# A two-layer hybrid backbone on one core: the places of layer 1's experts, its output rows, and the making of the first mixer's input

## The chip, the core and the metric

The kernel runs on one core of one Trainium2 chip, in one launch. The metric is the device time of that core in microseconds (us), the median of three runs. The engines are named as the profile names them: PE (TensorE, matrix products and transposes), DVE (VectorE), ACT (ScalarE), POOL (GpSimd) and SP (SyncE, which here issues the loads of the weights). PEld is the loading of a stationary operand into PE.

## The reference, cut to what matters

Two layers; layer 0 mixes with a gated recurrence, layer 1 with attention, and each is followed by a mixture of 16 experts of which every token takes two. Layer 0 works on 512 tokens (256 of the context and 256 of the image), layer 1 on the 256 of the image.

```python
def modulate(x, g, shift, scale):
    return rms_norm(x, g) * (1 + scale) + shift

def rglru_mixer(hx, hc, in_w, ...):            # layer 0; hx, hc are outputs of modulate
    gx_, ux = jnp.split(hx @ in_w, 2, axis=-1)
    ...
    log_a = -LRU_C * r * jax.nn.softplus(-lam) # lam: a learned vector, the same for all tokens
    ...

def grouped_moe(h, router_w, router_b, w1, w3, w2):
    probs = jax.nn.softmax(h @ router_w + router_b, axis=-1)
    ...                                        # the best of 4 groups, its best two experts
    y = jnp.zeros_like(h)
    for e in range(N_EXPERTS):
        y = y + gates[..., e:e + 1] * ((jax.nn.silu(h @ w1[e]) * (h @ w3[e])) @ w2[e])
    return y

# layer 1, last line
x = x + g_f * grouped_moe(hx, router_w, router_b, moe_w1[i], moe_w3[i], moe_w2[i])
```

D_MODEL is 1024, the experts' inner width 512. One weight matrix of one expert is 2 MB, so an expert is 6 MB in three tiles (w1, w3, w2).

## The kernel before, in words

**Weights.** SP issues all weight loads in a fixed list, each tile in two halves of 1 MB, with at most four halves in flight (`AHEAD`). A tile of weights goes into one of ten buffers in layer 1; `done(key)` gives a tile's buffer up and sends the next load of the list.

**Layer 1's experts** (`moe_`, `run`). The experts are worked one after the other at places 0 to 15, called `e` in the code. Places 0 to 3 hold experts 0 to 3, whose weights can be loaded before the router is done. The other twelve are ranked by how many tokens they got, and `ORDERS[1]` says which rank stands at which place from 4 on. `ROOM[1]` gives each rank its room: 160 rows for ranks 0 and 1, 32 for the rest, and `AGAIN` marks ranks 2 and 3, which get a further block of 128 rows under an `If` when they have over 32 tokens. Room of 160 is two blocks, one of 128 tokens and one of 32. From the reference, with these inputs, the router gives the places from 4 on 32, 29, 147, 19, 147, 16, 7 and 1 tokens; from place 12 on there are none, and their loads and work are skipped. No `If` finds over 32 tokens.

At each place PE does, in this order: `ups(e)` (w1 and w3, then the turning of the next expert's tokens), `downs(e-1)` (w2 of the place before), `flips(e)` (the transposes ahead of its own `downs`), and, if the next place has two blocks, the turning of its second block (`xh`). At place 11 `downs(10)` comes ahead of `ups(11)`. After `ups(e)` the buffers of w1 and w3 are given up, after `downs(e-1)` that of w2.

**Output rows.** `down` scales the product out of PSUM by gate and gain with DVE (L989) into a piece of `ys`, two tiles of 1024 columns (they are rows of the buffer `xr`), and POOL adds the piece to the output in DRAM by an indirect DMA (L995), a scatter. `row` picks the piece: a block of 128 rows takes the whole of `ys[(e + b) % 2]`, a block of 32 rows takes 256 columns of `ys[e % 2]`. A write into a piece waits until the scatter that reads the same bytes has landed. Each scatter waits until the one before it has landed, and holds POOL's queue meanwhile.

**The first mixer's input** (`modulate`). For each of 8 groups of 128 channels `k`, `m` is scale times value plus shift for 512 tokens, `hi` is `m` rounded to the narrower type `fp32r` and `lo` is what is left over, also in that type; PE then makes three products for each `k` (`mm3`: L182 with both high parts, L183 with `lo`, L184 with the low part of the weights). `m` is made by ACT, or by DVE where k is 1, 4 or 7; `hi` by DVE; `lo` by DVE or, for odd k, by POOL. `split` parts the weights in the same way: high part by DVE (L584), low part by POOL (L585). `lambda_terms` makes three small vectors out of `lam` with some thirty DVE instructions on 128x16 numbers and one `Exp` of ACT; the recurrence uses them for the first time in `back(0)`. In this stretch the order of PE, ACT and DVE is the order in which the code is written.

Of the kernel before, what the change touches and what calls it, by code (L numbers as in the profile page):

```python
# [12 lines left out]
AF = mybir.ActivationFunctionType  # L13
ALU = mybir.AluOpType
# [20 lines left out]
ADA_AT = [32, 34]  # L35


ORDERS = [[11, 0, 10, 1, 9, 2, 8, 3, 7, 4, 6, 5, 12], [2, 3, 0, 4, 1, 5, 6, 7, 8, 9, 10, 11]]
ROOM = [[192, 128, 96, 96, 96, 96, 64, 64, 64, 64, 64, 64, 32], [160, 160, 32] + 9 * [32]]

AGAIN = [[1, 2, 3, 4, 6], [2, 3]]
# [25 lines left out]
def base(i, k):  # L67

    return BASE if k < FIRST[i] else ROOM[i][ORDERS[i][k - FIRST[i]]]


def again(i, k):

    return k < FIRST[i] or ORDERS[i][k - FIRST[i]] in AGAIN[i]

# [12 lines left out]
def hybrid_kernel(ctx: ExitStack, tc: tile.TileContext, x, c, ctxt, c_ctx, ada_w, ada_b, norm_mix_w, norm_ffn_w,  # L88
# [3 lines left out]
    nc = tc.nc  # L92
# [77 lines left out]
    def take(key):  # L170
        return live[key][0]
# [106 lines left out]
    def vectors():  # L278
        pt = bank()
        nc.tensor.transpose(pt[:, 0:128], v1, ident)  # L280
        nc.tensor.transpose(pt[:, 128:256], v2, ident)
        nc.vector.tensor_copy(vt, pt[:, 0:256])
        init.close()
# [10 lines left out]
    def tables(pool):  # L294
        stage = pool.tile([128, C_COS - C_N], F32, name="stage", bufs=1)
        nc.gpsimd.dma_start(cst[:, 128:C_N], cf[:, 128:C_N])
        nc.gpsimd.dma_start(stage, cf[:, C_N:C_COS])
        nc.gpsimd.dma_start(rot, cf[:, C_COS:C_ALL])
        nc.gpsimd.dma_start(rw, router_w.rearrange("(k p) e -> p k e", p=128))
        nc.gpsimd.dma_start(rb, router_b.unsqueeze(0).to_broadcast([128, E]))  # L300
        nc.gpsimd.dma_start(qkw[:, 0, :], attn_q_norm_w.to_broadcast([128, 64]))
        nc.gpsimd.dma_start(qkw[:, 1, :], attn_k_norm_w.to_broadcast([128, 64]))
        for dst, at in ((lt_b, C_LT), (io_b, C_IO), (dup_b, C_DUP)):
            nc.vector.tensor_copy(dst, stage[:, at - C_N:at - C_N + dst.shape[1]])
        nc.vector.memset(ones_b, 1.0)
# [34 lines left out]
    def vec(i, m):  # L340
        return adT[i][:, m * 8:m * 8 + 8, :]

    def scale_vec(i, m, gain0, name):
        t = cp.tile([128, NK, 2], F32, name=name)
        g = vt[:, gain0 + i * 8:gain0 + i * 8 + 8].unsqueeze(2).to_broadcast([128, NK, 2])
        nc.vector.scalar_tensor_tensor(t, vec(i, m), 1.0, g, ALU.add, ALU.mult)
        return t
# [37 lines left out]
    def modulate(pool, xT, hi, lo, between):  # L385

        A = scale_vec(0, SC_M, 96, "am0")
        B = vec(0, SH_M)
        for k in range(NK):
            m = pool.tile([128, 512], F32, tag="m", name="m", bufs=3)  # L390
            for j in range(2):
                sl = slice(j * 256, j * 256 + 256)
                if k % 3 == 1:
                    nc.vector.tensor_scalar(m[:, sl], xT[:, k, sl], A[:, k, j:j + 1], B[:, k, j:j + 1], ALU.mult, ALU.add)
                else:
                    nc.scalar.activation(m[:, sl], xT[:, k, sl], AF.Identity, bias=B[:, k, j:j + 1], scale=A[:, k, j:j + 1])
            if k == 0:
                between()
            nc.vector.tensor_copy(hi[:, k, :], m)  # L399
            (nc.gpsimd if k % 2 else nc.vector).tensor_sub(lo[:, k, :], m, hi[:, k, :])  # L400

    yr0 = dp.tile([512, D], F32, name="yr0")

# [145 lines left out]
    def lambda_terms():  # L549
        nl, w, s, s2 = (sw[:, a, :] for a in range(4))  # L550
        nc.vector.tensor_scalar(nl, lam, -1.0, None, ALU.mult)
        nc.vector.tensor_tensor(w, nl, lam, ALU.min)
        nc.scalar.activation(w, w, AF.Exp)
        nc.vector.tensor_scalar(s, w, 2.0, None, ALU.add)
        nc.vector.reciprocal(s, s)
        nc.vector.tensor_mul(s, s, w)
        nc.vector.tensor_mul(s2, s, s)
        nc.vector.memset(k8, 1.0 / 17)
        for q in range(15, 0, -2):
            nc.vector.tensor_mul(k8, k8, s2)  # L560
            nc.vector.tensor_scalar(k8, k8, 1.0 / q, None, ALU.add)
        nc.vector.tensor_mul(k8, k8, s)
        nc.vector.tensor_scalar(k8, k8, 2.0, None, ALU.mult)
        nc.vector.tensor_scalar(nl, nl, 0.0, None, ALU.max)
        nc.vector.tensor_add(k8, k8, nl)
        nc.vector.tensor_scalar(k4, k8, 4.0, None, ALU.mult)
        nc.vector.tensor_scalar(k8n, k8, -8.0, None, ALU.mult)

    with tc.tile_pool(reuse_waits="tile", name="big0", bufs=1) as bp:
# [9 lines left out]
        def split(name, b):  # L579

            w = take((name, b // 4)).rearrange("p (k f) -> p k f", k=NK)[:, :, (b % 4) * 128:(b % 4) * 128 + 128]
            at = 2048 * (name == "ing")
            h, lo = (parts[:, at + z * 1024:at + (z + 1) * 1024].rearrange("p (k f) -> p k f", k=NK) for z in range(2))
            nc.vector.tensor_copy(h, w)  # L584
            nc.gpsimd.tensor_sub(lo, w, h)  # L585
            whi[name, b] = h, lo
            if b % 4 == 3:
                done((name, b // 4))
# [10 lines left out]
        with tc.tile_pool(reuse_waits="tile", name="n0", bufs=2) as n0, \  # L599
                tc.manual_schedule(engines={ET.PE, ET.Activation, ET.DVE}):  # L600
            ras = []
            normed(n0, yT, lambda: ras.append(ada_mm(0, 0, False)), lambda: None)
            ras.append(ada_mm(0, 1, False))
            vectors()
            for n in range(2):
                ada_sum(0, n, ras[n])

            hhi = wp.tile([128, 4096], F32R, tag="w", name="hhi").rearrange("p (k t) -> p k t", k=NK)
            parts = wp.tile([128, 4096], F32R, tag="w", name="parts")
            lambda_terms()  # L610
            ras = [ada_mm(0, n) for n in (2, 3)]
            for n in range(2):
                ada_sum(0, 2 + n, ras[n])
            modulate(n0, yT, hhi, hlo, lambda: split("in", 0))
            split("ing", 0)
            split_gates(0)
        with tc.tile_pool(reuse_waits="tile", name="m0", bufs=1) as mp:
# [64 lines left out]
            u = front(0)  # L682
            pg = product("ing", 0)
            split("in", 1)
            tables(mp)
            for b in range(8):
                r = gate_mm(b, *u[1:])
# [48 lines left out]
    def moe_(R, rp, early):  # L736
# [15 lines left out]
        if i == 0:  # L752
            xg, xh, sx, ys = places()
        with tc.tile_pool(reuse_waits="tile", name=f"r{i}", bufs=1) as q:
# [37 lines left out]
            m = small([128, C * E], "m")  # L792
# [47 lines left out]
        if i == 1:  # L840
            R.gf = rp.tile([128, D], F32, name="gf")
            xg, xh, sx, ys = places()
# [119 lines left out]
        def row(e, b, bk):  # L962

            if i == 1 and BLOCKS[bk] == BLOCKS[2]:

                return ys[e % 2][:, e // 2 % 4 * 256:]
            return ys[(e + b) % 2] if i or b == 0 else ys[2]

        def down(bk, aT, W2, ls, b, e):
# [699 lines left out]
def _constants():  # L1669
# [30 lines left out]
    for i in range(2):  # L1700
        k = FIRST[i]
        a[:, C_KEY + 16 * i:C_KEY + 16 * i + 16] = np.where(x < k, 65536 + 16384 * (k - 1 - x), E - 1 - x)
        a[:, C_RANK + 16 * i:C_RANK + 16 * i + 16] = list(range(k)) + [k + r for r in ORDERS[i]]
        a[:, C_ROOM + 16 * i:C_ROOM + 16 * i + 16] = [room(i, k) for k in range(E)]
# [32 lines left out]
```

## Time and profile before

| | us |
|---|---|
| median of three runs | 1001.43 |
| lowest and highest | 999.87, 1001.97 |
| the profiled execution, its own time | 1000.39 |
| its span, first to last instruction | 998.7 |
| PE busy | 854.6 (86%) |
| DVE, ACT, POOL busy | 488.5, 300.3, 253.8 |

The mean granted clock of PE is 0.933 of full speed. How to read the rows below: a row of the timeline has the start in us from the span's start, the time in us (of all its instructions together, pauses under 0.15 us included), engine, line, operation, out<-in, shape, count, and in brackets the idle time of the engine ahead of it and what ended it. Shapes tell the blocks of layer 1 apart: `128*128` is a block of 128 tokens, `128*64` one of 64, `128*32` one of 32. PE's lines in layer 1 are L946 (`ups`), L981 (`downs`), L928 (turning tokens), L958 (`flips`).

### The profile page before, as it was taken

Reading aid. Unit: us, or ns where it says so; the run is one execution under the profiler, and the core shown is the slowest. Engines: PE = TensorE matmul, PEld = TensorE weight load, DVE = VectorE, ACT = ScalarE, POOL = GpSimd, SP = SyncE. Lnnn points to the kernel's source line nnn. Section 1 sums busy time; section 2 is a strip of 40 time slices with the busy share of each in tenths; the row PEclk is TensorE's granted clock in tenths of the full one; section 3 lists DMA queues with packets and bytes.
Section 4 is the critical chain, followed back from the end, with each engine's and each line's share of the span. In section 5 each row is a group of like instructions: output and inputs, shape, how many; then the busy total and the mean of one; then the engine's idle time right before and its main releaser. Section 6 shows DMA issues by size and latency. Waiting matters only on the chain. (4 is left out here: it accounts for less than half of the span.)

```text
span 998.7 us, 17124 instructions
## 1 busy us (share of the span) xinstructions
PE 854.6 (86%) x6495; PEld 541.9 (54%) x6495; DVE 488.5 (49%) x1366; ACT 300.3 (30%) x549; POOL 253.8 (25%) x193
## 2 busy tenths in 40 slices
PE   3789899889996999999998953899999689799963
PEld 2356676575454555555654523688654556555632
DVE  1878797643147731222131106687842674334542
ACT  3346555674021211010011012557851311111100
POOL 2263233400002321111121106652430122313222
PEclk9799999998997999999999976799999799999987
DMA  9955974799515699999999985222949579999950
GB/s 346 357 175 191 389 264 169 261 386 380 211 67 213 239 361 385 363 363 359 351 337 372 374 288 175 84 73 80 354 162 399 204 290 370 378 386 367 382 184 9
DMA packets 126926, 277.11 MB, mean 277 GB/s; under 512 B 7673, under 2 KB 12889, under 8 KB 126816
## 3 DMA queue, kind: packets, MB, share of 16 engines
q1 hardware_dynamic: 116064, 253.77, 69.3%
q0 software_dynamic: 8880, 15.54, 6.7%
q10 hardware_dynamic: 1872, 6.37, 1.6%
q8 instruction: 64, 1.05, 0.4%
q14 instruction: 46, 0.38, 0.1%
HBM read 290.85 MB, written 14.81 MB: 306 GB/s over the span
## 5 line engine op out<-in xcount | busy, mean ns | idle before, releaser
L946 PE MATMUL up<-w,xg 128*64 128x256 f32 (+2 forms) x1888 | 171.7, 345 | 9.9 <-DMA w<-in_moe_w_dram 8.9
L946 PEld LDWEIGHTS up<-w,xg 128*64 128x64 f32 (+2 forms) x1888 | 107.2, 128 | 67.3 <-issue 31.8
L981 PE MATMUL py<-w,sx 128*32 128x256 f32 (+2 forms) x768 | 129.9, 528 | 6.0 <-DVE sx L960 3.4
L951 DVE TENSOR_TENSOR sx<-sx,up 128x256 f32<-128x256 f32 (+3 forms) x31 | 15.3, 494 | 174.3 <-PE up L946 97.5
L981 PEld LDWEIGHTS py<-w,sx 128*32 128x32 f32 (+2 forms) x768 | 45.7, 137 | 71.3 <-issue 55.8
L950 ACT ACTIVATE sx<-up 128x256 f32<-128x256 f32 (+3 forms) x31 | 12.2, 394 | 232.5 <-PE up L946 232.5
L585 POOL TENSOR_TENSOR parts<-w,parts 128x1024 fp32r<-128x1024 f32 x16 | 40.4, 2525 | 113.2 <-DVE parts L584 105.2
L995 POOL DMA_INDIRECT yr<-y,yi x21 | 33.4, 1591 | 121.4 <-DVE y L992 54.3
L531 PE MATMUL bank<-w,yT 128*128 128x512 f32 x128 | 57.3, 595 | 0.0
L182 PE MATMUL bank<-hhi,parts 128*128 128x512 f32 x128 | 52.9, 413 | 3.9 <-DVE hhi L399 3.8
L183 PE MATMUL bank<-hlo,parts 128*128 128x512 f32 x128 | 52.5, 410 | 4.2 <-DVE hlo L400 2.2
L184 PE MATMUL bank<-hhi,parts 128*128 128x512 f32 x128 | 51.9, 406 | 1.3 <-POOL parts L585 1.3
L918 POOL DMA_INDIRECT xg<-hr,gi x21 | 20.8, 991 | 125.9 <-DVE f L909 74.9
L946 PE MATMUL up<-w,xr 128*32 128x128 f32 (+2 forms) x736 | 51.2, 315 | 1.4 <-issue 0.9
L316 PE MATMUL bank<-w,st 128*32 128x512 f32 x384 | 46.5, 615 | 3.8 <-DMA w<-in_ada_w_dram 3.5
L946 PEld LDWEIGHTS up<-w,xr 128*32 128x32 f32 (+2 forms) x736 | 35.5, 120 | 14.5 <-issue 9.5
L933 ACT ACTIVATE xg<-tp 128x512 f32<-128x512 f32 x32 | 17.4, 594 | 84.7 <-PE tp L928 72.2
L992 DVE TENSOR_SCALAR y<-py,gt 128x512 f32<-128x512 f32 (+1 forms) x21 | 14.4, 687 | 56.7 <-PE py L981 55.1
L989 DVE SCALAR_TENSOR_TENSOR xr<-py,gt,gf 32x256 f32<-32x256 f32 (+2 forms) x44 | 24.4, 554 | 35.0 <-DMA out_dram<-xr,yi 19.6
L465 DVE TENSOR_TENSOR rt<-bank,gm 128x512 f32<-128x512 f32 x12 | 8.3, 692 | 66.9 <-PE bank L531 66.9
L531 PEld LDWEIGHTS bank<-w,yT 128*128 128x128 f32 x128 | 23.4, 190 | 25.7 <-issue 25.5
L1610 POOL TENSOR_SCALAR pe<-pe,mx 128x512 f32<-128x512 f32 x16 | 25.0, 1566 | 45.0 <-DVE mx L1605 29.7
(360 smaller groups left out, 1635.9 us busy)
## 6 DMA issues: line engine op xcount, KB each, us to landing
w<-in_moe_w_dram SPq DMA_DIRECT2D x192, 1024.0 KB
w<-in_ada_w_dram SPq DMA_DIRECT2D x48, 1024.0 KB
w<-in_lru_in_w_dram SPq DMA_DIRECT2D x8, 1024.0 KB
w<-in_attn_qkv_w_dram SPq DMA_DIRECT2D x6, 1024.0 KB
w<-in_lru_out_w_dram SPq DMA_DIRECT2D x4, 1024.0 KB
w<-in_attn_o_w_dram SPq DMA_DIRECT2D x4, 1024.0 KB
hr<-h ACTq DMA_DIRECT2D x6, 512.0 KB
yr<-zero POOLq DMA_DIRECT2D x4, 512.0 KB, 12.4
```

The source lines that it names most:

```text
L182: nc.tensor.matmul(pb, wh, xh, start=start, stop=False, skip_group_check=True)
L183: nc.tensor.matmul(pb, wh, xl, start=False, stop=False, skip_group_check=True)
L184: nc.tensor.matmul(pb, wl, xh, start=False, stop=stop, skip_group_check=True)
L316: nc.tensor.matmul(pa[32 * g:32 * g + 32, :], st[:, 4 * r + g, :], w[:, 4 * r + g, :], start=r == 0, stop=r == 1, skip_group_check=True, t ...
L531: nc.tensor.matmul(pb, src[:, k, n * 128:(n + 1) * 128], w[:, k, :], start=k == 0, stop=k == NK - 1)
L585: nc.gpsimd.tensor_sub(lo, w, h)
L918: nc.gpsimd.indirect_dma_start(out=dst[0:rows, :], out_offset=None, in_=hr[:, :], in_offset=bass.IndirectOffsetOnAxis(ap=idx[0:rows, :], a ...
L946: nc.tensor.matmul(pw[g * Tn:(g + 1) * Tn, at:at + fg], hT[:, k, t0:t0 + Tn], W[:, k, g * fg:(g + 1) * fg], start=k == 0, stop=k == NK - 1 ...
L981: nc.tensor.matmul(py[j * Tn:(j + 1) * Tn, 0:wd], aT[:, ao + q * 128 + g * Tn:ao + q * 128 + (g + 1) * Tn], W2[:, f, j * dg + h * 512:j * ...
L989: nc.vector.scalar_tensor_tensor(dst[ps, :], py[ps, 0:wd], gate[ps, :], R.gf[ps, at:at + wd], ALU.mult, ALU.mult)
L995: nc.gpsimd.indirect_dma_start(out=yr[:, :].rearrange("r (g f) -> (r g) f", g=G), out_offset=bass.IndirectOffsetOnAxis(ap=ls.yi[:, z, b:b ...
L1610: (nc.gpsimd if u else nc.vector).tensor_scalar(pe, pe, mx[:, 1:2], None, ALU.mult)
```

## The change

Four edits. `ORDERS[1]` begins with 2, 0, 3, 1, 4 instead of 2, 3, 0, 4, 1: places 4 to 8 now hold 32, 147, 29, 147 and 19 tokens. A block of 32 rows takes `ys[(e + b) % 2]`, so that the second block of an expert goes into the other tile than its first. In `modulate` ACT writes `hi` directly, DVE makes `m` for every k and all of `lo`; POOL makes none of it. `lambda_terms()` is called later in the code, behind the second `split("in", ...)`.

```diff
-ORDERS = [[11, 0, 10, 1, 9, 2, 8, 3, 7, 4, 6, 5, 12], [2, 3, 0, 4, 1, 5, 6, 7, 8, 9, 10, 11]]
+ORDERS = [[11, 0, 10, 1, 9, 2, 8, 3, 7, 4, 6, 5, 12], [2, 0, 3, 1, 4, 5, 6, 7, 8, 9, 10, 11]]
...
             for j in range(2):
                 sl = slice(j * 256, j * 256 + 256)
-                if k % 3 == 1:
-                    nc.vector.tensor_scalar(m[:, sl], xT[:, k, sl], A[:, k, j:j + 1], B[:, k, j:j + 1], ALU.mult, ALU.add)
-                else:
-                    nc.scalar.activation(m[:, sl], xT[:, k, sl], AF.Identity, bias=B[:, k, j:j + 1], scale=A[:, k, j:j + 1])
+                nc.scalar.activation(hi[:, k, sl], xT[:, k, sl], AF.Identity, bias=B[:, k, j:j + 1], scale=A[:, k, j:j + 1])
+                nc.vector.tensor_scalar(m[:, sl], xT[:, k, sl], A[:, k, j:j + 1], B[:, k, j:j + 1], ALU.mult, ALU.add)
             if k == 0:
                 between()
-            nc.vector.tensor_copy(hi[:, k, :], m)
-            (nc.gpsimd if k % 2 else nc.vector).tensor_sub(lo[:, k, :], m, hi[:, k, :])
+            nc.vector.tensor_sub(lo[:, k, :], m, hi[:, k, :])
...
-            lambda_terms()
             ras = [ada_mm(0, n) for n in (2, 3)]
...
             split("in", 1)
+            lambda_terms()
             tables(mp)
...
-                return ys[e % 2][:, e // 2 % 4 * 256:]
+                return ys[(e + b) % 2][:, e // 2 % 4 * 256:]
```

DVE at the start of the first mixer, before: the last of `lambda_terms` (L566, L567) is behind it; the last two `ada_sum` (L329, L330) and the scale vector `am` (L346) come first, then the first `split` and `modulate`.

```order
44 L329 TENSOR_REDUCE rs<-bank 128x8
45 L330 TENSOR_TENSOR adT_133<-rs,vt 128x8
46 L329 TENSOR_REDUCE rs<-bank 128x8
47 L330 TENSOR_TENSOR adT_133<-rs,vt 128x8
48 L346 SCALAR_TENSOR_TENSOR am_344<-adT_133,vt 128x16
49 L584 CAST parts<-w 128x1024
50 L399 CAST hhi<-m 128x512
51 L400 TENSOR_TENSOR hlo<-m,hhi 128x512
52 L394 TENSOR_SCALAR m<-yT,am_344,adT_133 128x256 x2
```

The same place after the change, with the lines three lower (L557 to L564 are now the end of `lambda_terms`, L581 the `split`, L397 `lo`).

```order
39 L329 TENSOR_REDUCE rs<-bank 128x8
40 L557 TENSOR_TENSOR k_140<-k_140,sw 128x16
41 L330 TENSOR_TENSOR adT_133<-rs,vt 128x8
42 L558 TENSOR_SCALAR k_140<-k_140 128x16
43 L346 SCALAR_TENSOR_TENSOR am_314<-adT_133,vt 128x16
44 L559 TENSOR_TENSOR k_140<-k_140,sw 128x16
45 L394 TENSOR_SCALAR m<-yT,am_314,adT_133 128x256 x2
46 L560 TENSOR_SCALAR k_140<-k_140 128x16
47 L562 TENSOR_TENSOR k_140<-k_140,sw 128x16
48 L563 TENSOR_SCALAR k_142<-k_140 128x16
49 L564 TENSOR_SCALAR k8n<-k_140 128x16
50 L581 CAST parts<-w 128x1024
```

The scheduler has not moved `lambda_terms` behind the products, as the code reads, but spread it between the `ada_sum` instructions, and `am` no longer stands behind all of it; the rounding of `hi` (L399) is gone from DVE.

PE at place 5 of layer 1, before: one block of 32 rows, then the `If` for more (L1150) and the turning of place 6.

```order
2723 L946 MATMUL up<-w,xg_13405 32x128 x64
2724 L1150 COMPARE_AND_BRANCH
2725 L928 MATMUL tp<-cst,xh 128x128 x8
2726 L946 MATMUL up<-w,xh 128x512 x16
2727 L958 MATMUL py<-cst,sx_13408 128x128 x4
2728 L1150 UNCONDITIONAL_BRANCH x2
2729 L928 MATMUL tp<-cst,xr 128x128 x8
```

The same place after the change.

```order
2719 L925 MATMUL tp<-cst,xh 128x128 x8
2720 L1089 TENSOR_LOAD cnk
2721 L1089 ISA x2
2722 L943 MATMUL up<-w,xg_13413 128x512 x16
2723 L943 MATMUL up<-w,xh 32x128 x64
2724 L925 MATMUL tp<-cst,xr 128x128
2725 L1020 UNCONDITIONAL_BRANCH
2726 L925 MATMUL tp<-cst,xr 128x128 x7
```

The expert with two blocks now stands here, and the `If` has gone to place 6.

POOL at the end of layer 1, before: the two scatters of place 8 (a row of 1024 columns, then pieces of 256), with gathers of later places between, then those of places 9, 10 and 11.

```order
2561 L995 DMA out_dram<-xr,yi 256x1024
2562 L995 DMA out_dram<-xr,yi 1024x256
2563 L1011 MEMSET xr 128x1024
2564 L918 DMA xr<-hr_13190,gi 32x1024
2565 L995 DMA out_dram<-xr,yi 1024x256 x2
2566 L1011 MEMSET xg_13405 128x1024
2567 L918 DMA xg_13405<-hr_13190,gi 32x1024
2568 L995 DMA out_dram<-xr,yi 1024x256
```

The same place after the change: the two scatters are now those of place 7.

```order
2555 L992 DMA out_dram<-xr,yi 256x1024
2556 L992 DMA out_dram<-xr,yi 1024x256
2557 L1008 MEMSET xr 128x1024
2558 L915 DMA xr<-hr_13198,gi 32x1024
2559 L992 DMA out_dram<-xr,yi 1024x256
2560 L1008 MEMSET xr 128x1024
2561 L915 DMA xr<-hr_13198,gi 32x1024
2562 L992 DMA out_dram<-xr,yi 1024x256 x2
2563 L1008 MEMSET xg_13413 128x1024
2564 L915 DMA xg_13413<-hr_13198,gi 32x1024
2565 L992 DMA out_dram<-xr,yi 1024x256
```

One more scatter and one more gather stand behind the last expert with two blocks.

## Rows read from the trace of the kernel before

**Rows 1.** Stretches of layer 1: start:end, length, busy by engine, PEclk, DMA, GB/s.

```profile
860.00:960.00 100.00, 92.60 (x1152) 56.18 (x1151) 39.54 (x151) 15.68 (x44) 25.40 (x22) 0.97 1.04 377
960.00:965.00 5.00, 0.03 (x2) 0.03 (x2) 2.34 (x7) 0.30 (x1) 0.20 (x1) 0.64 0.29 80
965.00:985.00 20.00, 15.37 (x239) 9.24 (x238) 11.92 (x55) 0.28 (x1) 8.34 (x7) 0.76 0.10 12
```

**Rows 2.** Timeline of PE, places 5 to 8 of layer 1.

```profile
865.49 4.18 PE L946 MATMUL up<-w,xg 128*32 128x128 f32 x128
...
872.60 1.30 PE L928 MATMUL tp<-cst,xr 128*128 128x128 f32 x5 [1.87 <-issue]
...
879.68 13.90 PE L946 MATMUL up<-w,xr 128*128 128x512 f32 x32
...
908.65 8.98 PE L981 MATMUL py<-w,sx 128*128 128x512 f32 x48
...
937.23 1.93 PE L981 MATMUL py<-w,sx 128*32 128x256 f32 x32
```

**Rows 3.** Timeline of PE, places 10 and 11 and the end.

```profile
954.30 3.82 PE L946 MATMUL up<-w,xr 128*32 128x128 f32 x128
...
964.97 0.22 PE L898 MATMUL pa<-r,dup_b 128*128 128x5 bf16 x3 [5.82 <-DVE r L883]
965.12 3.45 PE L981 MATMUL py<-w,sx 128*32 128x256 f32 x32
...
971.19 3.24 PE L981 MATMUL py<-w,sx 128*32 128x256 f32 x32 [2.33 <-DVE sx L960]
...
978.03 0.91 PE L946 MATMUL up<-w,xg 128*32 128x128 f32 x23 [0.30 <-issue]
...
981.61 3.41 PE L981 MATMUL py<-w,sx 128*32 128x256 f32 x32
```

**Rows 4.** Timeline of DVE: the second block of place 8.

```profile
962.56 1.96 DVE L989 SCALAR_TENSOR_TENSOR xr<-py,gt,gf 32x256 f32<-32x256 f32 x4 [9.55 <-DMA out_dram<-xr,yi]
```

**Rows 5.** Scatters: one link of the chain, then landings within 860:960 and from 960.

```profile
953.28 9.15 DMA out_dram<-xr,yi
...
DMA to landing us min/median/max: 7.4/7.4/7.5
...
DMA to landing us min/median/max: 3.8/3.8/3.9
```

**Rows 6.** Timeline of POOL: the last scatter.

```profile
987.50 1.59 POOL L995 DMA_INDIRECT out_dram<-xr,yi  x1 [6.07 <-DVEq L1233]
```

**Rows 7.** Timeline of all engines at the start of the first mixer.

```profile
34.49 0.66 PE L327 MATMUL bank<-cst,ra 128*128 128x128 f32 x4 [0.19 <-ACT ra L321]
...
37.04 0.18 DVE L346 SCALAR_TENSOR_TENSOR am<-adT,vt 128x16 f32<-128x16 f32 x1
...
37.68 0.69 DVE L584 CAST parts<-w 128x1024 fp32r<-128x1024 f32 x1 [0.47 <-DMA w<-in_lru_in_w_dram]
...
38.52 2.49 POOL L585 TENSOR_TENSOR parts<-w,parts 128x1024 fp32r<-128x1024 f32 x1 [32.28 <-DVE parts L584]
...
38.84 2.72 DVE L400 TENSOR_TENSOR hlo<-m,hhi 128x512 fp32r<-128x512 f32 x1
...
41.48 0.72 DVE L394 TENSOR_SCALAR m<-yT,am,adT 128x256 f32<-128x256 f32 x2
...
41.65 1.09 ACT L396 ACTIVATE m<-yT,adT,am 128x256 f32<-128x256 f32 x2 [2.32 <-DVE hlo L400]
...
47.15 0.69 DVE L400 TENSOR_TENSOR hlo<-m,hhi 128x512 fp32r<-128x512 f32 x1
...
51.41 1.67 POOL L400 TENSOR_TENSOR hlo<-m,hhi 128x512 fp32r<-128x512 f32 x1 [1.74 <-DVE hhi L399]
...
51.84 1.51 DVE L593 CAST g<-w 128x512 fp32r<-128x512 f32 x1
...
53.88 0.60 ACT L628 ACTIVATE upad<-bank 128x512 f32<-128x512 f32 x1 [6.25 <-PE bank L184]
```

## The prediction

> **What bounds the kernel now.** I read the share of the engines first, then the stretches of layer 1, then PE's timeline there, and last the start of the first mixer. PE is busy for 86% of the span, so an edit counts only where PE, or what follows its last product, waits. In layer 1 the stretches say which resource ends last [rows 1]: from 860 to 960 us the transfers run at 377 GB/s with a DMA share of 1.04 while PE is busy for 92.6 of 100 us; at 960 the weights are in (80 GB/s, then 12). Yet PE goes on until 985. So after 960 neither the weights nor PE's rate is the limit: between 960 and 965 PE is busy for 0.03 us, and between 965 and 985 for 15.4 us at a granted clock of 0.76. The rows of PE name the reasons. It waits 5.82 us for DVE, then 2.33 us more [rows 3], and its `downs` of one block of 32 rows, 1.93 us at place 7 [rows 2], take 3.45, 3.24 and 3.41 us [rows 3], as much longer as the level of 1.2 GHz in place of 2.4 over part of them makes them; the engine had idled ahead of each. DVE was late because the second block of place 8 is written into columns that the scatter of the first block is still reading: 9.55 us of waiting [rows 4], and the scatter takes 9.15 us [rows 5].
>
> Why PE is that late at all is in [rows 2, 3]: an expert with two blocks costs PE some 30 us (13.9 + 3.7 of `ups`, 9.0 of `downs`, 2.2 of turning), one with 32 rows some 7.5 us, and a tile of 2 MB comes every 5.6 us at 377 GB/s, and I take 5.8, since gathers and scatters share that rate, so an expert's weights every 17.4 us. PE falls behind at places 6 and 8 and catches up at the light ones; before, only places 9 to 11 are left for it.
>
> **Edit 1, the order of ranks in layer 1.** PE's instructions are the same, each in another place. I lay them out from 865.5 us, where place 5 begins [rows 2]; up to there nothing changes but the `xh` gather, which is issued one place earlier. Durations are those of the rows; small steps of 0.3 to 1.1 us (turns, flips, index products) are in the sums.
> - Place 5, now two blocks: turn of `xh`, then 17.5 us of `ups` (13.90 for the first block [rows 2], 3.7 for the second): 866.5 to 884. Turn, `downs(4)`, flips: 890.
> - Place 6: 3.8 us, the `If` that came with rank 3 and some 1.5 us of idling around it (before, 1.87 at place 5 [rows 2]), turn, `downs(5)` 9.0 (8.98 [rows 2]), `xh`: 907.
> - Place 7: 17.5, turn, `downs(6)` 1.93, flips: 928.4.
> - Place 8: 3.8, turn, `downs(7)` 9.0, flip: 943.
> - Place 9: 3.8 [rows 3], turn, 1.93, flip: 950.3. Place 10 the same: 957.5.
> - `downs(10)` waits for its flips through DVE, 2.1 us (2.33 before [rows 3]), and takes 1.9: 961.6. `ups(11)`: 965.4. The handing over through ACT and DVE took from 978.94 to 981.61 [rows 3], 2.7 us: 968.2. `downs(11)` between 1.93 and 3.41, I take 2.7: **970.9**, against 985.0 now [rows 3], a gain of 14.1 us.
> What follows the last product stays: the scatter at 987.50 [rows 6] and the end, 13.7 us behind 985.0. The weights allow it: ten tiles are held, and counted back from 960 at 5.8 us each the last three land at about 949, 955 and 961, so that `ups(11)` (second half from 963.5) and `downs(11)` (968.2) find theirs. They are the lower end: `downs(11)` can't end before some 965, a gain of 20. The upper end is PE catching up nothing: only the 5.82 and 2.33 us go, 8.2.
>
> The price on the other side is that a heavy place holds its tiles longer. The `ups` of place 7 would give up w1 and w3 at 924.5, when six tiles are still to be sent; what was sent before lands by about 926 (six times 5.8 before 961), so the loads just don't run dry. A dry pipe costs nothing until it has moved the last tile by some 7 us.
>
> **Edit 2, the rows of the output.** The second block now writes the other tile. That one was last read by the scatter of the place before, sent at about 930 (place 6) for a write at 943: 13 us for a scatter of 7.4 to 9.15 [rows 5]. The wait of 9.55 us [rows 4] is gone, and so is its twin behind place 6, which lay under 17 us of `ups` and cost nothing. What is late next is POOL: scatters still go one by one. From the first of place 7 at 941.3 I add 9.15 and twice 7.4 while weights are loaded, then twice 3.8 [rows 5]: the fifth has landed at 972.9, and the last product's rows are ready at 973.4. So this chain has half a microsecond to spare; 0 to 3 us are the bounds of what it adds, I take 0.
>
> **Edit 3, `modulate`.** Removed: DVE's 8 roundings and POOL's four subtractions (1.67 us the last of them [rows 7]). Added: ACT makes both halves of `hi` for all k, 8 times 1.09 us [rows 7], which lies beside DVE's work; DVE needs 0.72 for `m` and 0.69 for `lo` [rows 7], 1.41 us for each k. Today the product ends at 53.88 [rows 7]. After: the weights' high part still starts at 37.68, since it waits for its load [rows 7]; `lo` for k = 0 follows at 38.4; POOL's low part then takes 2.49 us [rows 7], to about 41.5, while DVE's next `m` waits; then seven k at 1.41 us end at 51.4, and the last two products at 52.3, 1.5 us earlier. The second `split` starts only 0.8 us earlier, since today DVE does its roundings between.
> What DVE and POOL do to each other is seen in [rows 7]: with POOL's subtraction from 38.52 to 41.01, DVE's takes 2.72 us in place of 0.69, and at 51.41 POOL's takes 1.67, behind one DVE instruction, while the next DVE instruction of 51.84 takes 1.51. POOL thus gets its turn after one instruction.
> The Trainium skill, "SBUF — State Buffer", section "Who interferes with whom", says that a DVE instruction with two SBUF inputs, or in a 2-port mode, and a GpSimd instruction that reads SBUF block each other fully, and that issue order decides who is blocked. By that rule, DVE issuing without a pause could keep POOL out; the sum would then be the rival on the port below, and by the row at 51.41 it is the one above.
>
> **Edit 4, `lambda_terms`.** It costs the same instructions, but now spread out, so that `am` follows the last transposes (done at 35.15 [rows 7]) at about 35.6 and not 37.04 [rows 7]. ACT starts 1.4 us earlier; the weights' load at 37.68 takes that back for the first product. Edits 3 and 4 together: 0.8 us, between 0 (the loop behind takes it back) and 1.5.
>
> **Sum.** Span 998.7 − 14.1 − 0.8 = 983.8. The profiled execution took 1000.39, 1.69 us over its span, and lies 1.04 under the median of the three runs: 985.5 as that execution, 986.5 as the median; I say 986.
>
> **Rivals.**
> - *The wait goes, the catching up does not.* Light places follow each other every 7.5 us, and each hands work to DVE, ACT and POOL and back; if that stalls PE again, with a lower clock behind it as in [rows 3], only the two waits are gained, 8.2 + 0.8: 992. For it: all five rows from 964 on wait or are slow. Against it: places 5 to 7 ran without such waits while PE was behind.
> - *DVE keeps POOL off the port.* Then the low part of the first weights comes after DVE's eleven us, and PE, which works in order, does 22 products behind it: the product ends near 62, 8 us later than now. Time 994. Against it: the row at 51.41.
> - *The chain of scatters takes the place of the wait, and ends slower.* If the five links behind 941.3 take 9.15 us each to the end [rows 5], the last is sent at 987, as now: 999.5, no change. With a memset and a gather of POOL between (1.9 us), 11 us a link, it is sent at 996: 1008, slower. It decides from about 9.2 us a link. For it: POOL's order and 9.15 at 953. Against it: 3.8 from 960 on [rows 5], when the weights are in.
> - *The change doesn't do what it says*: were DVE's wait kept on the whole buffer, place 8's flips would wait for place 7's first scatter until 951, and PE 5 us: 991, with the first rival.
>
> **Chances.** The forecast (982 to 990) 0.60; the first rival and the kept wait 0.22; the port 0.04; the chain without change 0.09 and slower 0.05. A measurement of this kernel can tell about 0.2%, 2 us. Faster 0.86, within 0.2% 0.09, slower 0.05. The range goes from 981.5 (the weights' bound: 20 us less) to 994, the rivals on the port and on catching up; the chain is left out.
>
> **What would show it.** Right: no DVE L986 of 32 rows waits for the output's DMA behind places 5 and 7; PE's last `downs` at 968 to 974 with a clock above 0.9 from 930 to 960; the weights in by 960 to 963; `upad` of the first mixer near 53. Wrong: a dry pipe between 900 and 930; scatters in the tail over 7 us each; the last scatter sent behind 980; POOL's first subtraction ending behind 45.

## The result, and the profile after

The changed kernel took 992.26 us (median of 6 runs), the kernel before, run beside it, 1000.74: a ratio of 0.9922, with a 95% interval of 0.9900 to 0.9944. That is faster, by 8 us (0.8%); the forecast was 986, which is 14.7 us under the kernel beside it. The profiled execution took 991.52 us with a span of 989.9, 8.8 less than before, where 14.9 were forecast.

The stretches of layer 1 after the change (start:end, length, PE's busy time, granted clock, DMA share, GB/s; before in [rows 1]):

```profile
900.00:930.00 30.00, 27.60 (x294) 0.99 1.03 357
930.00:960.00 30.00, 28.13 (x507) 0.96 0.99 357
960.00:965.00 5.00, 2.00 (x26) 0.82 0.17 18
965.00:976.00 11.00, 9.21 (x193) 0.81 0.11 14
```

The weights are in by 960 as before, loads never run dry between 900 and 930, and PE is done at 976 instead of 985. But between 960 and 976 it is busy for 11.2 of 16 us, again with pauses and at a clock of 0.8. PE's timeline at places 5 to 8 (the middle rows of [rows 2], in the new order):

```profile
863.09 1.06 PE L925 MATMUL tp<-cst,xh 128*128 128x128 f32 x8 [2.39 <-DMA xh<-hr,gi]
863.99 15.60 PE L943 MATMUL up<-w,xg 128*128 128x512 f32 x32
...
889.18 0.33 PE L955 MATMUL py<-cst,sx 128*128 128x128 f32 x1 [2.22 <-DVEq L1163]
...
893.77 1.10 PE L925 MATMUL tp<-cst,xr 128*128 128x128 f32 x8 [0.51 <-DVEq L1147]
...
904.81 13.90 PE L943 MATMUL up<-w,xr 128*128 128x512 f32 x32
...
928.31 0.33 PE L955 MATMUL py<-cst,sx 128*128 128x128 f32 x1 [2.22 <-DVEq L1163]
...
928.60 5.37 PE L943 MATMUL up<-w,xg 128*32 128x128 f32 x128
```

L1147 and L1163 are the two `If`s of an expert that may have more rows (in `ups` and in `downs`). The flips of places 5 and 7 stand behind the `If` in `downs` of places 4 and 6 and wait 2.22 us each. In the first of these waits DVE scales the product of place 4, and PE goes on 0.1 us behind it:

```profile
887.11 1.97 DVE L986 SCALAR_TENSOR_TENSOR xr<-py,gt,gf 32x256 f32<-32x256 f32 x4
```

Behind pauses the same products take longer: 15.60 us at place 5 for the 13.90 of place 7, 5.37 at place 8 for 3.70 at place 9. And the end, which answers to [rows 3]:

```profile
944.10 3.70 PE L943 MATMUL up<-w,xr 128*32 128x128 f32 x128
...
957.00 0.30 PE L943 MATMUL up<-w,xr 128*32 128x128 f32 x1 [1.64 <-issue]
...
963.59 3.42 PE L978 MATMUL py<-w,sx 128*32 128x256 f32 x32 [2.93 <-DVE sx L957]
966.84 3.67 PE L943 MATMUL up<-w,xg 128*32 128x128 f32 x128
...
972.97 3.19 PE L978 MATMUL py<-w,sx 128*32 128x256 f32 x32
```

The wait of 5.82 us is gone; a wait ahead of `downs(10)` (2.93 now, 2.33 before), a pause in which PE waited for nothing that the profile shows (1.64), and two slow `downs` (3.42 and 3.19 us for 1.93) are there. DVE's second blocks, which answer to [rows 4], and POOL's last scatters ([rows 6]):

```profile
904.32 1.97 DVE L986 SCALAR_TENSOR_TENSOR xr<-py,gt,gf 32x256 f32<-32x256 f32 x4 [1.64 <-PE ls L876]
...
944.40 1.97 DVE L986 SCALAR_TENSOR_TENSOR xr<-py,gt,gf 32x256 f32<-32x256 f32 x4 [1.59 <-PE ls L876]
```

```profile
971.83 1.56 POOL L992 DMA_INDIRECT out_dram<-xr,yi  x1 [4.04 <-PE ls L876]
978.63 1.59 POOL L992 DMA_INDIRECT out_dram<-xr,yi  x1 [3.04 <-DVEq L1230]
```

No second block waits for the output's DMA any more, and the last scatter is sent 2.5 us after PE's end, as before. The first mixer ([rows 7]):

```profile
38.42 2.67 POOL L582 TENSOR_TENSOR parts<-w,parts 128x1024 fp32r<-128x1024 f32 x1 [32.18 <-DVE parts L581]
```

```profile
38.80 2.77 DVE L394 TENSOR_SCALAR m<-yT,am,adT 128x256 f32<-128x256 f32 x2
```

```profile
51.91 0.60 ACT L624 ACTIVATE upad<-bank 128x512 f32<-128x512 f32 x1 [8.82 <-PE bank L184]
```

`upad` comes 2.0 us earlier than before, and the first gate product, at 61.35 us for 62.76, 1.4.

### The profile page after: what moved, and what is told of

Same layout as the page of the kernel before. It is cut to its first block, busy times and chain, and to the rows that moved or that the text cites. A ratio compares the mean times of both kernels' runs of the same rounds, so it can differ in the third digit from the quotient of the medians.

```text
span 989.9 us, 17139 instructions
## 1 busy us (share of the span) xinstructions
PE 848.3 (86%) x6495; PEld 536.3 (54%) x6495; DVE 489.8 (49%) x1372; ACT 302.8 (31%) x555; POOL 247.4 (25%) x189
## 5 line engine op out<-in xcount | busy, mean ns | idle before, releaser
L943 PE MATMUL up<-w,xg 128*64 128x256 f32 (+2 forms) x1888 | 173.8, 350 | 9.7 <-DMA w<-in_moe_w_dram 9.0
L943 PEld LDWEIGHTS up<-w,xg 128*64 128x64 f32 (+2 forms) x1888 | 108.6, 130 | 67.7 <-issue 32.2
L978 PE MATMUL py<-w,sx 128*32 128x256 f32 (+2 forms) x768 | 127.2, 513 | 5.9 <-DVE sx L957 4.0
L182 PE MATMUL bank<-hhi,parts 128*128 128x512 f32 x128 | 52.3, 409 | 4.0 <-DVE parts L581 4.0
L183 PE MATMUL bank<-hlo,parts 128*128 128x512 f32 x128 | 52.3, 409 | 2.0 <-DVE hlo L397 1.9
L992 POOL DMA_INDIRECT out_dram<-xr,yi x14 | 22.1, 1581 | 50.9 <-DVEq L1163 11.9
```

The source lines that it names most:

```text
L182: nc.tensor.matmul(pb, wh, xh, start=start, stop=False, skip_group_check=True)
L183: nc.tensor.matmul(pb, wh, xl, start=False, stop=False, skip_group_check=True)
L943: nc.tensor.matmul(pw[g * Tn:(g + 1) * Tn, at:at + fg], hT[:, k, t0:t0 + Tn], W[:, k, g * fg:(g + 1) * fg], start=k == 0, stop=k == NK - 1 ...
L978: nc.tensor.matmul(py[j * Tn:(j + 1) * Tn, 0:wd], aT[:, ao + q * 128 + g * Tn:ao + q * 128 + (g + 1) * Tn], W2[:, f, j * dg + h * 512:j * ...
L992: nc.gpsimd.indirect_dma_start(out=yr[:, :].rearrange("r (g f) -> (r g) f", g=G), out_offset=bass.IndirectOffsetOnAxis(ap=ls.yi[:, z, b:b ...
```

## Experiments

Twelve runs of ten kernels, in three series. The kernel before took 1000.74 us beside the result above, 995.98 in the first series, 999.63 and 998.43 in the second and third, so times are compared within a series, and across series only as ratios. One more number is used: the **layer-1 stretch**, from the end of the flips of place 4 (PE's last L955, or L958 before) to the end of the last `downs`, both read from PE's timeline. It is 119.5 us before (865.5 to 985.0) and 115.5 after (860.7 to 976.2). Profiles with the same layer 1 differ in it by up to 2.4 us, so smaller differences say nothing: it is 119.5 and 117.4 with the old order and rows (`before`, `mixer_only`), and 115.3 to 117.7 in the five profiles with the new ones (`after`, `after_again`, `after_3`, `order_rows`, `order_rows_2`). On average that is 2.3 us less; the 4.0 of the first pair lies near the upper end of what such pairs give.

My theory at first (A): the two waits are gone, but light places still cost hand-overs. The rival (B): layer 1 brings most of the 8.8 us, and the rest is chance.

**The parts alone** (first series).

`mixer_only`, edits 3 and 4:

```
-ORDERS = [..., [2, 0, 3, 1, 4, 5, 6, 7, 8, 9, 10, 11]]
+ORDERS = [..., [2, 3, 0, 4, 1, 5, 6, 7, 8, 9, 10, 11]]
-                return ys[(e + b) % 2][:, e // 2 % 4 * 256:]
+                return ys[e % 2][:, e // 2 % 4 * 256:]
```

> Edits 3 and 4 alone; layer 1's order and rows as in the kernel before. In the trace of the changed kernel layer 1's first product of the experts starts at 793.53 us, in that of the kernel before at 797.07: 3.5 us of the 8.8 us that the span lost are there before layer 1's experts begin, although the forecast gave these edits 0.8 us. Theory A (the edits bring this, since the loop behind the mixer's input does not take it back but adds to it): ratio 0.9960 to 0.9975, 2.5 to 4 us. Theory B (the 3.5 us are the difference of two executions; the edits are worth what they were forecast): ratio 0.9985 to 0.9995, 0.5 to 1.5 us. Both: upad of the first mixer near 52 us.

995.5 us, ratio 0.9998 (0.9986 to 1.0011). Theory A's 2.5 us are ruled out. No gain can be measured; the median is 0.5 us lower, the lower end of B, and the interval leaves B open up to 1.4 us.

`order_rows`, edits 1 and 2 on the kernel before:

```
-ORDERS = [..., [2, 3, 0, 4, 1, 5, 6, 7, 8, 9, 10, 11]]
+ORDERS = [..., [2, 0, 3, 1, 4, 5, 6, 7, 8, 9, 10, 11]]
-                return ys[e % 2][:, e // 2 % 4 * 256:]
+                return ys[(e + b) % 2][:, e // 2 % 4 * 256:]
```

> Edits 1 and 2 alone (order and rows). Theory A: the light places lose again what the forecast had them catch up, so layer 1 brings only 5 to 6 us, ratio 0.9940 to 0.9950. Theory B: layer 1 brings most of the 8.8 us, 7.5 to 8.5 us, ratio 0.9915 to 0.9925. The forecast's own term was 14.1 us, ratio 0.986.

993.04 us, 0.9966 (0.9951 to 0.9982): 3 us, below both here. In the third series the same kernel has 0.9943, within A.

`order_only`, edit 1:

```
-ORDERS = [..., [2, 3, 0, 4, 1, 5, 6, 7, 8, 9, 10, 11]]
+ORDERS = [..., [2, 0, 3, 1, 4, 5, 6, 7, 8, 9, 10, 11]]
```

> Edit 1 alone: the second block of places 5 and 7 is again written into columns that the first block's scatter reads. DVE should wait some 8 to 9 us for the output's DMA at about 904 and 944. Theory A (only the wait behind the last heavy place costs PE time, since the one at 904 lies under 17 us of products): PE waits 2 to 4 us for DVE at downs(8) or the flip before it, and the gain over the kernel before is 2 to 4 us smaller than that of order and rows together. Theory B (both are covered now, because PE has light places behind them and is late anyway): same time as order and rows together, within 1 us.

999.94 us, 1.0040 (1.0026 to 1.0053): slower than the kernel before, and 6.9 us behind order and rows together; A named the place, but not the size. DVE's second block of place 7, then PE:

```profile
953.62 1.97 DVE L989 SCALAR_TENSOR_TENSOR xr<-py,gt,gf 32x256 f32<-32x256 f32 x4 [10.21 <-DMA out_dram<-xr,yi]
```

```profile
956.04 0.22 PE L898 MATMUL pa<-r,dup_b 128*128 128x5 bf16 x3 [6.61 <-DVE r L883]
```

`rows_only`, edit 2:

```
-                return ys[e % 2][:, e // 2 % 4 * 256:]
+                return ys[(e + b) % 2][:, e // 2 % 4 * 256:]
```

> Edit 2 alone, in the old order (heavy places 6 and 8). The wait of 5.82 us at 964.97 of the kernel before is gone. Theory A (light places stall anyway, and the wait of 2.33 us and the half clock stay): 4 to 5.5 us, ratio 0.9945 to 0.996, so that with rows alone nearly all of layer 1's gain is there and the order adds 0 to 2 us. Theory B (the order is what brings the gain; without it POOL's chain of scatters ends last): 0 to 2 us, ratio 0.998 to 1.0.

994.02 us, 0.9979 (0.9964 to 0.9993): 2 us, as B says, but for another reason. DVE now waits one place later, and PE behind it:

```profile
965.11 1.97 DVE L989 SCALAR_TENSOR_TENSOR xr<-py,gt,gf 32x256 f32<-32x256 f32 x4 [4.59 <-DMA out_dram<-xr,yi]
```

```profile
967.45 3.64 PE L981 MATMUL py<-w,sx 128*32 128x256 f32 x32 [7.60 <-DVE sx L960]
```

With heavy places at even `e`, the second block of place 8 takes `ys[1]` from column 0, and place 9 takes the same columns. With heavy places 5 and 7 the second block takes the same columns as the place before it, whose scatter has landed by then: DVE's rows at 904.32 and 944.40 wait for PE alone. So these two edits need each other: −2 and +4 us alone, −3 together.

**The whole, and the rows alone in a form that can't meet** (second series).

`after_again`, the changed kernel as it is.

> The changed kernel as it is, beside the other kernels of this call. Orders and rows alone were measured at 0.9966, the mixer's edits alone at 0.9998, the whole change at 0.9922, in another series. Theory A (the parts add up, and the first series' kernel before was some 4 us slower on the whole than in the second): ratio 0.995 to 0.9975 here. Theory B (the parts help each other, as order and rows do): ratio 0.991 to 0.993 here too.

991.23 us, 0.9923 (0.9901 to 0.9945), as at first and as B says. That the parts help each other is not shown by it: `order_rows` has 0.9966 in one series and 0.9943 in another.

`rows_free`, on the kernel before:

```
-                return ys[e % 2][:, e // 2 % 4 * 256:]
+                return ys[(e + b) % 2][:, (e // 2 + 2 * b) % 4 * 256:]
```

> The old order (heavy places 6 and 8), with rows that never meet: a block of 32 rows takes ys[(e + b) % 2] and there the columns (e // 2 + 2 * b) % 4. With the rows of the change in the old order, place 9 writes the same columns as the second block of place 8, DVE waited 4.59 us at 965.11 for its scatter and PE 7.60 us for DVE. Theory A (what the new order brings is mostly that its two heavy places, 5 and 7, don't meet places 6 and 8 in those columns): the old order with free rows gains 3 to 5 us over the kernel before, as much as order and rows together (0.995 to 0.997), and no wait of DVE for the output's DMA is left in the tail. Theory B (the light places behind the heavy ones bring it): at most 2.5 us, as rows alone (0.9975 or above), the stall of place 10 staying in another form.

992.22 us, 0.9938 (0.9910 to 0.9966), 1 us behind the changed kernel of the same series, although neither the order nor the mixer is changed. Its stretch is 114.3 us. Theory A on the order holds: what the new order gives beyond free rows can't be measured. DVE has no wait for the output's DMA in the tail any more, and PE's longest wait there is:

```profile
962.13 3.31 PE L981 MATMUL py<-w,sx 128*32 128x256 f32 x32 [2.92 <-DVE sx L960]
```

`no_if`, on the changed kernel; it leaves out the further block of 128 rows of ranks 2 and 3, which no token uses here:

```
-AGAIN = [[1, 2, 3, 4, 6], [2, 3]]
+AGAIN = [[1, 2, 3, 4, 6], []]
```

> The changed kernel without the second chance of ranks 2 and 3 in layer 1 (AGAIN[1] is empty: the further block of 128 rows under an If is left out, which no token needs with these inputs). In the changed kernel PE's pauses of 2.70 us (place 4), 2.39 (the gather of xh that POOL sends only behind that If), 2.22 (flips of place 5, behind downs(4)), 0.51 and 2.22 (place 6, flips of place 7) stand in that chain, 10 us in all, and 15.60 for 13.90 and 5.37 for 3.8 us of products at the lower clock behind them. Theory A (PE is what ends last, and these pauses are the part of the forecast's catching up that was lost): 5 to 9 us faster than the changed kernel. Theory B (the light places in the tail hand over as slowly whenever they come, and weights land no earlier than 960): 0 to 3 us faster.

981.88 us, 0.9823 (0.9799 to 0.9847): 9.4 us faster than the changed kernel beside it. Theory A, with a little more than its upper end. The `If` and the block under it go together here, so the run doesn't tell the branch from what its block does to the program. PE's waits between 860 and 977 us, all of them, of the changed kernel (us in total, times, longest):

```profile
PE py L955 <- DVEq L1163: 4.4, 2, 2.2
PE py L978 <- DVE sx L957: 2.9, 1, 2.9
PE tp L925 <- DMA xh<-hr,gi: 2.4, 1, 2.4
PE up L943 <- issue: 1.8, 2, 1.6
PE pa L895 <- DVE r L880: 1.0, 1, 1.0
PE pa L955 <- DVE r L899: 0.8, 1, 0.8
PE tp L925 <- DVEq L1147: 0.5, 1, 0.5
PE pa L955 <- DVE f L906: 0.4, 2, 0.2
PE pa L955 <- PEq L1163: 0.2, 1, 0.2
```

Without the `If`s those on L1147 and L1163 are gone: PE sends the second block's flips of place 5 at 880.56, ahead of DVE's scaling of place 4 (881.01), and not behind it. Of the 2.4 us for `xh` 1.0 is left. In this order the wait was largely the `If`'s too (in `no_if_old_order` below PE waits 2.83 us for `xh` without any `If`). In the changed kernel POOL stands at place 4's `If` before it may make `xh` ready, which it doesn't without:

```profile
855.41 0.95 POOL L1015 MEMSET xh<- 128x1024 f32 x1 [4.05 <-PEq L1147]
```

```profile
851.09 0.96 POOL L1015 MEMSET xh<- 128x1024 f32 x1
```

With PE's pauses the slow products went: `up` of place 5 takes 13.90 us, not 15.60. The stretch is 857.6 to 963.9 us, 106.3. Then another thing ends last: POOL's scatters, each waiting for the landing of the one before:

```profile
961.97 1.93 PE L978 MATMUL py<-w,sx 128*32 128x256 f32 x32
```

```profile
959.65 1.57 POOL L992 DMA_INDIRECT out_dram<-xr,yi  x1 [4.43 <-DMA out_dram<-xr,yi]
964.72 1.56 POOL L992 DMA_INDIRECT out_dram<-xr,yi  x1 [3.50 <-DMA out_dram<-xr,yi]
...
970.00 1.59 POOL L992 DMA_INDIRECT out_dram<-xr,yi  x1 [1.52 <-DVEq L1285]
```

The last is sent 6.1 us behind PE's end, not 2.5: some 3.6 us of PE's gain are given back there. The span is 8.7 us shorter than that of the changed kernel's first profile: 3.0 ahead of the stretch, where PE had waited 2.70 us at place 4's `If`, and 9.2 in it (7.4 up to `ups(9)`, 1.8 behind it), less the 3.6.

`swap_last`, on the changed kernel:

```
-                last = lo == 0 and e == G - 1 < E - 1
+                last = False
```

> The changed kernel with ups(11) ahead of downs(10), as at every other place (last = False). In the changed kernel PE waits 2.93 us ahead of downs(10) for the flips to come back through DVE and then takes 3.42 us for 1.93 us of products; ups(11), 3.67 us, would lie in that gap. Theory A (the hand-over costs where nothing lies beside it): PE ends 4 to 5 us earlier, and the time falls by 3 to 4 us, since POOL's chain of scatters (966.21, 971.83, 978.63) then ends some 3.5 us earlier. Theory B (the same wait stands again ahead of downs(11), and the chain of scatters is what ends last): 0 to 1 us.

990.66 us, 0.9910 (0.9887 to 0.9933), 0.6 us less than the changed kernel: theory B in the time and in the wait, though the chain of scatters doesn't end last (the last is sent 2.5 us behind PE's end, as before). `ups(11)` fills the gap, and the waits come back behind it, now 2.07 and 2.99 us, with a slow last `downs`:

```profile
968.58 0.33 PE L955 MATMUL pa<-cst,sx 128*128 128x128 f32 x1 [2.07 <-DVE r L899]
...
971.93 0.22 PE L895 MATMUL pa<-r,dup_b 128*128 128x5 bf16 x3 [2.99 <-DVE r L880]
972.08 3.64 PE L978 MATMUL py<-w,sx 128*32 128x256 f32 x32
```

**The order again, without `If`s, and the mixer again** (third series).

`after_3`, the changed kernel.

> The changed kernel once more, to stand beside order_rows_2 on the same chip. It was 0.9922 and 0.9923 of the kernel before in two series. Both theories: 0.990 to 0.9945 if the kernel before is near 1000 us here as in those series, 0.995 to 0.997 if it is near 996 as in the series of the first four experiments.

990.38 us, 0.9918 (0.9887 to 0.9949).

`order_rows_2`, edits 1 and 2, with the diff of `order_rows`.

> Edits 1 and 2 alone, again. Theory A (the mixer's edits bring nothing that lasts): within 1 us of the changed kernel of this call. Theory B (the mixer's edits are worth the 1.0 to 1.4 us by which the loop behind the product starts earlier in the trace, and later stages keep it): 1.5 to 3 us slower than the changed kernel of this call.

993.51 us, 0.9943 (0.9923 to 0.9963). The medians differ by 3.1 us, B's upper end, the means of the runs by 1.5; the intervals overlap, and the first series gave the mixer's edits nothing.

`no_if_old_order`, on the changed kernel; the further block is left out as in `no_if`:

```
-ORDERS = [..., [2, 0, 3, 1, 4, 5, 6, 7, 8, 9, 10, 11]]
+ORDERS = [..., [2, 3, 0, 4, 1, 5, 6, 7, 8, 9, 10, 11]]
-AGAIN = [[1, 2, 3, 4, 6], [2, 3]]
+AGAIN = [[1, 2, 3, 4, 6], []]
-                return ys[(e + b) % 2][:, e // 2 % 4 * 256:]
+                return ys[(e + b) % 2][:, (e // 2 + 2 * b) % 4 * 256:]
```

> No Ifs in layer 1 (AGAIN[1] is empty, the further block of ranks 2 and 3 left out), the mixer as changed, rows that never meet, but the old order of places (heavy ones 6 and 8). The new order without Ifs took 981.88 us. Theory A (PE is busy without a gap from place 4 to 9 in either order, so an order of places can't make it end earlier): within 1.5 us of the 981.9. Theory B (with the Ifs gone, light places behind the heavy ones are worth something, since POOL's chain of scatters has longer to catch up behind place 7 than behind place 8): 3 to 6 us slower than 981.9.

983.35 us, 0.9840 (0.9810 to 0.9870), with a stretch of 108.6: by the ratios 1.7 us behind `no_if`, near A's bound, and the intervals overlap. PE isn't busy without a gap here, as theory A had it; one of its two longest waits in the stretch is that for `xh` of place 6:

```profile
865.77 1.94 PE L925 MATMUL tp<-cst,xh 128*128 128x128 f32 x8 [2.83 <-DMA xh<-hr,gi]
```

`no_if_4_6`, as the last, with heavy places 4 and 6:

```
-ORDERS = [..., [2, 3, 0, 4, 1, 5, 6, 7, 8, 9, 10, 11]]
+ORDERS = [..., [0, 2, 1, 3, 4, 5, 6, 7, 8, 9, 10, 11]]
```

> No Ifs in layer 1, as before, and the heavy places one further up, at 4 and 6, with rows that never meet. In the run without Ifs POOL sends the last five scatters at 943.65, 951.45, 959.65, 964.72 and 970.00, each behind the landing of the one before, while PE ends at 963.90: the chain ends last there. Theory B (the chain ends last, and one more light place lets it catch up): 2 to 4 us faster than 981.9. Theory A (the total of PE's work decides, the order doesn't): within 1.5 us. If heavy places hold their weight buffers so long that loads run dry, 2 us slower or more.

985.26 us, 0.9866 (0.9836 to 0.9896): not faster, 1.9 us over `no_if_old_order` beside it, an amount that the intervals don't part. The transfers slacken between 900 and 920, and the weights are in later than 965:

```profile
900.00:920.00 20.00, 19.81 (x330) 13.43 (x329) 7.32 (x28) 2.66 (x7) 5.44 (x5) 1.00 0.96 342
...
960.00:965.00 5.00, 4.49 (x127) 4.03 (x119) 2.11 (x8) 0.28 (x1) 0.83 (x1) 0.80 1.00 364
```

SP, which sends the loads, waits for PE's `up` to give up buffers, 12.4 us between 860 and 985, where it has no such wait in `no_if`, 0.2 us in `no_if_old_order` and 7.6 in the changed kernel; PE waits for weights only once, in its last `downs`:

```profile
SPq L159 <- PE up L943: 12.4, 4, 5.9
```

```profile
968.14 1.07 PE L978 MATMUL py<-w,sx 128*32 128x256 f32 x16 [0.29 <-DMA w<-in_moe_w_dram]
```

So the price that the prediction named, buffers held longer, is seen here on the loads. That it makes the 1.9 us is not shown: from the experts' first product to the last `downs` this profile takes 172.6 us, that of `no_if_old_order` 172.0. This execution is late ahead of layer 1: its experts start at 796.62 us, those of `no_if` at 793.77.

## Why the forecast was right in sign and too large

The measured 992.26 lies above the forecast's own 982 to 990, and within the range only because that goes up to the rivals at 994.

**Edit 2, the wait: right, with a condition that was missed.** DVE's wait of 9.55 us and PE's 5.82 are gone, and the chain of scatters doesn't end last. That the new rows only work in the new order was not seen: the collision of places 8 and 9 in `rows_only` can be read from `row` alone. That the other tile "was last read by the scatter of the place before", 13 us ahead, was worked out for the places as they are after the change, and holds there (place 6's scatter is sent at 928.47, the columns are written from 944.40).

**Edit 1, the order: the step that failed.** The forecast laid PE's steps out from 865.5 to 970.9, 105.4 us, for the 119.5 of [rows 2, 3]. Measured were 115.5. PE came to place 5 4.8 us earlier than before; set against the forecast moved by as much (all us):

| | forecast, 4.8 earlier | measured | behind |
|---|---|---|---|
| `ups(5)` starts | 861.7 | 863.99 | 2.3 |
| `ups(6)` starts | 885.2 | 889.47 | 4.3 |
| `ups(7)` starts | 902.2 | 904.81 | 2.6 |
| `ups(8)` starts | 923.6 | 928.60 | 5.0 |
| `ups(9)` starts | 938.2 | 944.10 | 5.9 |
| place 10 done | 952.7 | 960.63 | 7.9 |
| `downs(10)` done | 956.8 | 967.01 | 10.2 |
| `downs(11)` done | 966.1 | 976.16 | 10.1 |

Two terms were mis-sized. The `If`s of places 4 and 6 were priced at "some 1.5 us of idling around it", at place 6 alone. At them and at `xh` stand 2.39 + 2.22 + 0.51 + 2.22 = 7.3 us of waits and 1.70 + 1.67 = 3.4 us of slower products behind them, 10.7, of which 1.0 for `xh` stays without the `If`s. (Which products are the slow ones changes: in `after_3`, behind a wait of 2.31 us for `xh`, the first block of place 5 takes 13.90 us, and `ups` of places 6 and 8 take 5.37 each.) And the light places at the end, 27.9 us in the forecast from `ups(9)` on, took 32.1: the pause of 1.64 us, 2.93 for 2.1 us of waiting, and `downs` of 3.42 and 3.19 us for 1.9 and 2.7. Together 13.4 us too little; 3.3 come back, because some small steps were laid too wide, 1.9 of them at place 5 (6 us behind `ups(5)` for 4.1 without the wait). `no_if` shows the first term: with the `If`s away the stretch is 106.3 us, for 105.4 laid out. So the forecast was nearly that of a kernel without `If`s. That the two lie within a microsecond is partly luck: up to `ups(9)` `no_if` takes 76.0 us for 77.5 laid out, behind it 30.2 for 27.9, so the second term stays.

The price could have been read from the old trace. There the `If`s stand at places 4 and 5, and between the flips of place 4 and those of place 6 PE waits 0.51, 1.87 [rows 2], 1.32 and 1.41 us, 5.1 in all:

```profile
878.78 1.07 PE L928 MATMUL tp<-cst,xh 128*128 128x128 f32 x8 [1.32 <-DMA xh<-hr,gi]
...
903.18 0.33 PE L958 MATMUL py<-cst,sx 128*128 128x128 f32 x1 [1.41 <-DVEq L1166]
```

The prediction took only the 1.87 for the `If`, and what it held against its first rival, that places 5 to 7 ran without waits that stall PE, these rows don't bear out.

Behind this stands a wrong thought: that an order lets PE "catch up". In the old order none of PE's waits between 860 and 977 us was for weights, and its work is the same in any order, so an order can gain only waits and what they bring with them. All PE's waits in the stretch add up to 16.4 us before and 14.2 after: the 5.82 went, the 2.33 came back as 2.93, and those at the `If`s and `xh` grew from 5.1 to 7.3. `rows_free` and `no_if_old_order` agree: with rows that can't meet, the old order costs 1 to 1.7 us, which the runs don't tell from nothing, and `rows_free`, with the mixer as it was, is no slower by its ratio (0.9938) than `order_rows` (0.9966 and 0.9943). The first rival named this, that the catching up does not come. That 992.26 is its time, 992, is luck in part: it had 8.2 us gained in the stretch, where 4.0 were, and the rest came ahead of it.

**Edits 3 and 4: 0.8 us, between 0 and 1.5; not settled.** The profile agrees with the steps: POOL's low part follows one DVE instruction (38.42), `upad` at 51.91 for a forecast of 52.3 to 53, the gate product 1.4 us earlier. The rule on the port that the prediction weighed (the Trainium skill, "SBUF — State Buffer", section "Who interferes with whom") agrees with the trace as far as blocking goes: DVE's `m` took 2.77 us beside POOL's subtraction, for 0.73 without it, as DVE's subtraction with two inputs had taken 2.72 for 0.69 [rows 7]. (`m` reads one tile; whether it runs in a 2-port mode, as the rule would have it, no row shows.) That DVE keeps POOL out by issuing without a pause, the rival at 994, is refuted by the row at 38.42: POOL's subtraction starts there and ends at 41.09, and not behind DVE's whole row of work. How much of the 1.4 us reaches the end is open: −0.5 us between medians in the first series, −3.1 in the third, and the traces say why it can't be told better (below).

**The span's 8.8 us** are thus 4.0 in the layer-1 stretch (forecast 14.1) and 4.8 ahead of it, of which 1.4 are seen in the first mixer; the rest stands in stretches that the change does not touch, where executions of one program differ by some 2 us (below). For the time, edits 1 and 2 brought 3.4 and 5.7 us by the ratios of two series (0.9966 and 0.9943), the whole 8.

**What would show it:** the last `downs` at 968 to 974 (972.97), the weights by 960 to 963, no wait of a second block, and `upad` near 53 came as said. The clock above 0.9 from 930 to 960 came too (0.96). None of them shows the 6 us that were missing; that the last `downs` fell into its window is luck, since the 4.8 us gained ahead of place 5 hid half of the 9.6 that `downs(11)` started late.

The best kernel that ran is `no_if`, faster than both. It gives up the further block; by the code, tokens beyond the room then go to `leftover`, whose price no run here shows.

## What to carry to other kernels

An order of work can gain only the waits that it removes: before laying out a new order, add up the waits in the old stretch, and ask of each whether it goes, stays or moves with the piece of work that makes it. A branch can cost far more than its own instructions: here PE could not run ahead of DVE past it, and POOL's gather was sent late, so price it by the rows around it and not by its own. Two pieces that share a buffer must be checked for all pairs of places, since a rule on odd and even that frees one pair can tie the next.

## Unexpected

The time ahead of layer 1's experts moves by some 2 us between executions of one and the same program. The changed kernel's three profiles have the experts start at 793.53, 793.28 and 795.37 us. `order_rows` and `order_rows_2` are the same kernel too, yet in the first profile they start at 795.68 us and in the second at 793.84. Two early stretches (length, PE busy, clock, DMA share, GB/s) show where the two part; `order_rows`, then `order_rows_2`:

```profile
63.00:73.00 10.00, 9.84 (x36) 0.83 0.30 36
...
215.00:237.00 22.00, 20.33 (x149) 0.84 1.04 386
```

```profile
63.00:73.00 10.00, 10.00 (x48) 1.00 0.35 47
215.00:237.00 22.00, 21.38 (x151) 0.92 1.04 386
```

The mean granted clock is lower in the first: over a longer part of these stretches PE has the level of 1.2 GHz. DVE's instructions behind them come 1.1 us earlier in `order_rows_2` at 73 us, and 2.9 at 237. What lowers the clock in one execution and not in the other, the profiles don't show. A gain of a microsecond ahead of such a stretch can't be followed to the end in single profiles.
